# Linear attention's gate pair moved behind the other input pairs, and the output projection's Strassen gemms rearranged

## The chip, the cores and the metric

The kernel runs on one core of one Trainium2 chip. The metric is device time of one execution in microseconds; the kernel before took 1664.3 us (median of three runs, 1661.51 to 1664.69). The engines are PE (TensorE: matmuls and transposes), DVE (VectorE), ACT (ScalarE), POOL (GpSimd, which here mostly issues DMAs) and SP (SyncE, which only issues DMAs). Each engine works through its own list of instructions in order.

## What is computed

Two layers over 512 tokens of width 2048, float32. Each layer normalises its rows, multiplies by one wide input matrix, splits the columns between a linear-attention group (GLA, 4 heads) and a chunked-attention group (8 heads), gates each group, multiplies by one output matrix, normalises again and adds to the residual:

```python
def hybrid_layer(x, w_in, w_out, g_pre, g_post, w_alpha, b_alpha, g_gla, g_att, rel_bias):
    h = rmsnorm(x, g_pre)
    z = h @ w_in
    gq, gk, gv, gg, ga, aq, ak, av, ag = split_columns(z)
    log_a = jax.nn.log_sigmoid((ga @ w_alpha + b_alpha).astype(jnp.float32)) / GLA_TAU
    o_gla = gla_chunk_causal(gq.reshape(...), gk.reshape(...), gv.reshape(...), log_a.reshape(...))
    o_gla = rmsnorm(o_gla, g_gla.reshape(GLA_HEADS, GLA_DV)).reshape(B, S, D_GLA)
    o_gla = o_gla * jax.nn.silu(gg)
    o_att = chunk_band_attention(aq.reshape(...), ak.reshape(...), av.reshape(...), rel_bias)
    o_att = rmsnorm(o_att, g_att.reshape(ATT_HEADS, ATT_HD)).reshape(B, S, D_ATT)
    o_att = o_att * jax.nn.silu(ag)
    y = jnp.concatenate([o_gla, o_att], axis=-1) @ w_out
    return x + rmsnorm(y, g_post)
```

## The kernel before

*Matmuls.* Both projections are cut into blocks of 512 columns and run with operands split in a high and a low part (`split`, L105), three matmuls per product of tiles. A block over all four groups of 128 tokens takes 192 matmuls of 128x512 in the plain form (`std_gemm`). `fast_gemm` (L311) computes a pair of blocks by a Strassen-like scheme with 7 products of half size, 28 jobs of 12 matmuls, 336 in place of 384. `PROD` and `PROD_END` are the order of the jobs; "51" means product P5, chunk c=1 of the inner dimension. The products read tokens' half matrices or sums of them (S1 to S4); the sums are formed once, written to DRAM and read back into the ring `sa` when a job wants them.

*Jobs.* Every job has a weight tile, either one block's (512 KB, `raw` or `H`) or a sum of two formed on DVE (L180, L182). ACT casts it into `wh` (four buffers), DVE forms the rest `wl` (three buffers, L194). `ahead` prepares loads 5 jobs, casts 4 jobs and splits 3 jobs in advance of the matmuls.

*Side work.* Everything between the gemms (token sums, attention heads, GLA heads, output sums, finishing of rows) is written as generators in the list `tasks`; each gemm calls `pump` a given number of times per job (`rate`), and `until` pumps until a condition holds. These generators only set the order in which instructions are handed over; a scheduler of the framework then fixes the order on each engine. Side work on PE writes to the four PSUM banks of `ps_ax`; the gemms accumulate in the four of `ps_mm`. Small tiles come from `t2`, eight buffers.

*A layer.* Input blocks in this order: the attention gates AG0 and AG1 in plain form, then six Strassen pairs (`PAIRS`, L126): GG (the GLA gate), AV, two QK pairs, KQ of the GLA group, GV. The gates are passed through SiLU and stored to DRAM (`gate`, L710). The GLA heads (`Unit`) run after GV; each loads its gate tile (in `states`), multiplies while it evicts (L1121), is transposed on PE (L1131), scaled on ACT (L1142), stored (L1146) and split into an output operand. `output_sums` (L545) reads these halves back (L549, L553) and forms S1 to S4 for each chunk of the output's inner dimension (L527 to L536, `put` with the store at L518).

*The output.* Blocks 0 and 1 in plain form, blocks 2 and 3 (`W23`) as a Strassen pair with `end=True`, in which P2 has an accumulator of its own in two `ps_ax` banks. In layer 0 block 1 is cut: tokens 0 to 255 before the pair and 256 to 511 after it, so that the rows of the first half are finished under the last gemm. `finish` normalises and adds the residual rows; in layer 0 it also prepares the next layer's operands.

Of the kernel before, what the change touches and what calls it, by code (L numbers as in the profile page):

```python
# [15 lines left out]
P = 128  # L16
L = 2
# [16 lines left out]
def hybrid_trunk(  # L34
# [59 lines left out]
    sg_d = [[dram([S, 1024], f"sg{l}{h}") for h in range(2)] for l in range(L)]  # L94
# [31 lines left out]
    PAIRS = ((GG0, GG1), (AV0, AV1), (QK01, QK23), (QK45, QK67), (GK, GQ), (GV0, GV1))  # L126
    W23 = (NB_IN + 2, NB_IN + 3)
# [8 lines left out]
    class Job:  # L136
# [14 lines left out]
        def load(self):  # L151
            k, c, p, b0, b1 = self.kind, self.c, self.pair, self.b0, self.b1
            end = b0 == W23[0]
            top, bottom = (c + 4, c) if end else (c, c + 4)
            if k == "std":
                self.raw = self.fetch(rtile("raw"), b0, c)
            elif k == "P1":
                p["H", c] = self.fetch(rtile("H"), b0, top)
            elif k == "P5":
                p["r", c] = self.fetch(rtile("raw"), b1, top)  # L160
            elif k == "P6":
                p["r", c] = self.fetch(rtile("raw"), b1, bottom)
            elif k == "P7":
                p["r", c] = self.fetch(rtile("raw"), b0, top)
            elif k == "P2" or (k == "P4" and end):
                p["r", c] = self.fetch(rtile("raw"), b0, bottom)
            src = (so_d if end else sa_d)[self.l].get((LEFT.get(k), c))
            if src is not None and not (k == "P5" and b0 == GG0):
# [3 lines left out]
        def high(self):  # L172
# [3 lines left out]
            else:  # L176
                h, r = p["H", c], p.get(("r", c))
                src = h if k in ("P1", "P5", "P6", "P4") else r
                if k in ("P5", "P6") or (k == "P4" and self.b0 == W23[0]):
# [11 lines left out]
        def low(self):  # L191
# [5 lines left out]
            if self.kind == "P2" and self.b0 != W23[0]:  # L197
# [4 lines left out]
    for l in range(L):  # L202
# [39 lines left out]
    delayed = []  # L242

# [67 lines left out]
    def fast_gemm(l, pair, consume, rate=0.0, skip=0, feature_major=False, after=None, end=False, lag=0):  # L311
# [38 lines left out]
        def matmuls(job, k, c, ts):  # L350
            a = job.a
            if a is None:
                a = A[{"P1": (0, 0, c), "P2": (1, 0, c), "P4": (1, 1, c), "P5": ("S1", c)}[k]]
            out_ps = acc[target[k]]
            fresh = k in starts and c == 0
            for kk in range(2):
                if feature_major:
                    for ft in range(4):
# [3 lines left out]
                        ops = ((job.wh, 0), (job.wh, 1), (job.wl, 0))  # L362
                        for m, (lhs, part) in enumerate(ops):
# [5 lines left out]
                else:  # L369
                    for t in ts:  # L370
                        tok = slice(kk * 256 + t * P, kk * 256 + (t + 1) * P)
                        ops = ((0, job.wh), (0, job.wl), (1, job.wh))
                        for m, (part, rhs) in enumerate(ops):
# [60 lines left out]
    STAGE = ("g16", "g17", "g4", "g5", "g10")  # L434
    HOME = {("S1", c): tag for c, tag in enumerate(("g9", "g14", "g15", "g2"))}
    XS0 = (("g6", "g7"), ("g12", "g13"))
# [25 lines left out]
    def prep_half(l, half, xs):  # L462
# [10 lines left out]
        h_end = next((i for i, z in enumerate(stream) if z.l == l - 1 and z.b0 == W23[0] and z.kind == "P4"), 0) + 1  # L473
# [32 lines left out]
    def make_sums(dst, tags, parts, home={}, chunks=range(4)):  # L506
        stage = [0]

        def put(name, c, src):
# [8 lines left out]
            nc.gpsimd.dma_start(dst[name, c], flat(op))  # L518

# [162 lines left out]
    def load_forget_gate(l):  # L682
        wga = [slot(tag, [n, 96], F32R) for tag, n in (("g6", 10), ("g7", 6))]
# [24 lines left out]
    def layer(l):  # L708
        last = l == L - 1
        def gate(half, q, t, src, scale=1.0):  # L710
            dst = t2()
            nc.scalar.activation(dst, src, AF.Silu, scale=scale)
            nc.gpsimd.dma_start(sg_d[l][half][t * P : (t + 1) * P, q * W : (q + 1) * W], dst)

        def gate_evac(half, q):
            def f(o, ps):
                gate(half, q, o, ps)
            return f

        def gate_consume(j, h, t, src, comb):  # L720
            gate(0, j, 2 * h + t, settled(src, comb))
# [94 lines left out]
        def raw_evac(o, ps):  # L816
            gate(1, 0, o, ps, r0[:, o : o + 1])

        if l:
            std_gemm(l, AG0, (0, 1), CO, operand_in, gate_evac(1, 0), rate=1.2)  # L820
            tasks.append(token_sums(l))
            tasks.append(forget_gate())
            std_gemm(l, AG0, (2, 3), CO, operand_in, gate_evac(1, 0), rate=0.8)
            std_gemm(l, AG1, range(NT), CO, operand_in, gate_evac(1, 1), rate=1.3, lag=2)
# [550 lines left out]
```

## Time and profile before

| | us |
|---|---|
| median of three runs | 1664.3 |
| lowest and highest of them | 1661.51 and 1664.69 |
| span of the profiled execution, first to last instruction | 1661.4 |
| layer 0, gate pair (102.71 to 178.87) | 76.16 |
| layer 0, output block 0 (631.29 to 700.86) | 69.57 |
| layer 0, first half of block 1 | 21.76 |
| layer 0, pair of blocks 2 and 3 | 79.79 |
| layer 0, second half of block 1 (802.41 to 827.76) | 25.35 |
| layer 1, output blocks 0 and 1 (1462.01 to 1568.92) | 62.71 and 44.20 |
| layer 1, pair of blocks 2 and 3, to its last matmul (1649.23) | 80.31 |
| from there to the end | 12.21 |

The profiler gives no other time of the profiled execution than its span. Stages are cut at the first matmul of each gemm. In a row of windows the columns are the stretch, its length, then for each engine the time it was busy and the number of instructions, the granted TensorE clock, the share of the 16 DMA engines that was busy and the rate. In a row of groups the numbers are: count, total busy time, mean duration in ns, and the engine's idle time just before, with what ended it. In a timeline row they are start, length, engine, line, operation, output and inputs, with the idle time before in brackets. In a row of DMA issues the last number is the median time to landing.

### The profile page before, as it was taken

What the parts mean: (1) busy time and instruction counts of PE and PEld (TensorE: products, weight loads), DVE (VectorE), ACT (ScalarE), POOL (GpSimd) and SP (SyncE); (2) the same over time, 40 slices, a digit from 0 to 9 for tenths busy, and PEclk for the clock granted to TensorE, in tenths of its full rate; (3) what the DMA queues carried; (4) which work ended last, traced back from release to release, by engine and by line L of the source; (5) the groups of instructions that cost most, each with busy time, mean ns of one, the idle gap of its engine ahead of it and who ended that gap; (6) DMA issues with size and microseconds to landing.
All of it is one profiled execution on the core that took longest, in us unless ns stands there. A gap on an engine that the chain in (4) does not pass through costs nothing.

```text
span 1661.4 us, 24811 instructions
## 1 busy us (share of the span) xinstructions
PE 1631.3 (98%) x9034; PEld 1393.9 (84%) x9034; DVE 1223.0 (74%) x1603; ACT 873.0 (53%) x1441; POOL 166.5 (10%) x252
## 2 busy tenths in 40 slices
PE   9999999999999999899999999999999999999996
PEld 7888889999988877688788888799999888777884
DVE  5977777787767876678886577667878678754778
ACT  7544544465665544454874445344656655343552
POOL 0110000000101101310122000000001011012103
PEclk9999999999999999999999999999999999999999
DMA  8898785858758777898789487868587687865975
GB/s 341 275 344 309 276 328 207 313 173 308 253 207 297 260 297 253 319 340 304 266 289 390 165 323 267 322 203 300 178 307 253 208 289 265 325 211 197 360 281 207
DMA packets 143722, 457.39 MB, mean 275 GB/s; under 512 B 15524, under 2 KB 32292, under 8 KB 143600
## 3 DMA queue, kind: packets, MB, share of 16 engines
q1 hardware_dynamic: 120848, 376.32, 63.9%
q0 software_dynamic: 22176, 78.41, 12.2%
q8 instruction: 71, 1.16, 0.3%
q10 hardware_dynamic: 576, 1.08, 0.2%
q14 instruction: 51, 0.42, 0.1%
HBM read 383.64 MB, written 72.11 MB: 274 GB/s over the span
## 4 chain that ended last, share of the span: by engine, by line
PE 85%; issue 6%; DMA 4%; DVE 3%; ACT 1%; POOL 1%; SPq 0%; DVEq 0%; POOLq 0%; ACTq 0%
PE mm L374 37%; PE mm L297 19%; PE mm L364 18%; PE ax L915 2%; DMA raw<-in_w_dram 2%; DVE wl L194 1%; PE ax L1069 1%; PE ax L898 1%; PE ax L1103 1%; PE ax L734 1%; DMA sa<-S 1%; PE ax L374 1%; DMA oS<-g 1%; PE ax L879 1%; PE ax L878 1%
## 5 line engine op out<-in xcount | busy, mean ns | idle before, releaser
L374 PE MATMUL mm<-wh,sa 128*128 128x512 f32 x1472 | 471.0, 392 | 3.2 <-DMA sa<-S 3.2
L186 ACT CAST wh<-raw 128x1024 fp32r<-128x1024 f32 (+1 forms) x249 | 260.8, 1051 | 273.0 <-PE mm L374 67.7
L194 DVE TENSOR_TENSOR wl<-raw,wh 128x1024 fp32r<-128x1024 f32 (+1 forms) x249 | 302.3, 1218 | 96.3 <-PE mm L374 37.1
L186 ACT CAST wh<-H 128x1024 fp32r<-128x1024 f32 x224 | 234.8, 1051 | 217.8 <-PE mm L374 98.7
L194 DVE TENSOR_TENSOR wl<-H,wh 128x1024 fp32r<-128x1024 f32 x224 | 273.3, 1222 | 86.8 <-PE mm L374 30.9
L374 PEld LDWEIGHTS mm<-wh,sa 128*128 128x128 f32 x1472 | 276.3, 188 | 62.7 <-DMA sa<-S 2.5
L374 PE MATMUL mm<-wl,sa 128*128 128x512 f32 x736 | 287.9, 391 | 0.0
L364 PE MATMUL mm<-sa,wh 128*128 128x256 f32 x1280 | 236.6, 285 | 0.0
L364 PEld LDWEIGHTS mm<-sa,wh 128*128 128x128 f32 x1280 | 199.5, 191 | 0.2
L374 PE MATMUL mm<-wh,a 128*128 128x512 f32 x576 | 189.7, 393 | 0.0
L364 PE MATMUL mm<-sa,wl 128*128 128x256 f32 x640 | 181.6, 284 | 0.6 <-DVE wl L194 0.6
L374 PEld LDWEIGHTS mm<-wl,sa 128*128 128x128 f32 x736 | 138.3, 188 | 28.5 <-issue 0.8
L180 DVE TENSOR_TENSOR H<-H,raw 128x1024 f32<-128x1024 f32 x120 | 145.7, 1221 | 9.3 <-DMA raw<-in_w_dram 8.2
L297 PE MATMUL mm<-wh,a 128*128 128x512 f32 x448 | 148.2, 395 | 3.1 <-ACT a L106 2.2
L416 POOL TENSOR_TENSOR sm<-sm,mhalf 128x2 f32<-128x2 f32 (+2 forms) x42 | 58.8, 1402 | 676.9 <-DVE sm L925 458.2
L374 PEld LDWEIGHTS mm<-wh,a 128*128 128x128 f32 x576 | 107.5, 188 | 21.8
L364 PEld LDWEIGHTS mm<-sa,wl 128*128 128x128 f32 x640 | 122.5, 191 | 1.2 <-DVE wl L194 1.0
L182 DVE TENSOR_TENSOR raw<-H,raw 128x1024 f32<-128x1024 f32 x56 | 68.6, 1225 | 73.1 <-DMA raw<-in_w_dram 72.8
L374 PE MATMUL mm<-wl,a 128*128 128x512 f32 x288 | 113.6, 394 | 0.0
L297 PEld LDWEIGHTS mm<-wh,a 128*128 128x128 f32 x448 | 83.8, 188 | 23.3 <-ACT a L106 2.6
L297 PE MATMUL mm<-wh,g 128*128 128x512 f32 x272 | 95.0, 398 | 2.2 <-ACT g L106 2.2
L297 PE MATMUL mm<-wh,sa 128*128 128x512 f32 x288 | 96.1, 396 | 1.0 <-ACT wh L186 0.6
(219 smaller groups left out, 2421.4 us busy)
## 6 DMA issues: line engine op xcount, KB each, us to landing
raw<-in_w_dram SPq DMA_DIRECT2D x311, 512.0 KB, 5.3
sa<-S SPq DMA_DIRECT2D x184, 512.0 KB, 4.4
H<-in_w_dram SPq DMA_DIRECT2D x56, 512.0 KB, 5.3
sa<-A SPq DMA_DIRECT2D x48, 512.0 KB, 5.9
S<-g POOLq DMA_DIRECT2D x32, 512.0 KB, 9.6
sa<-oS SPq DMA_DIRECT2D x32, 512.0 KB, 5.0
oS<-g POOLq DMA_DIRECT2D x24, 512.0 KB, 7.5
sg<-t POOLq DMA_DIRECT2D x32, 256.0 KB, 6.3
```

The costliest lines, as they stand in the source:

```text
L180: nc.vector.tensor_tensor(out=h, in0=h, in1=r, op=ALU.add)
L182: nc.vector.tensor_tensor(out=r, in0=h, in1=r, op=ALU.subtract)
L186: last_cast[0] = nc.scalar.copy(self.wh[:, z, :], src[:, z, :]).ins
L194: nc.vector.tensor_tensor(out=self.wl[:, z, :], in0=self.src[:, z, :], in1=self.wh[:, z, :].bitcast(F32), op=ALU.subtract)
L297: nc.tensor.matmul(pss[o], a(part, kk, o) if callable(a) else a[:, part, t], rhs[:, kk, :], start=(i == 0 and kk == 0 and m == 0), stop=(i ...
L364: nc.tensor.matmul(dst, lhs[:, kk, f], a[:, part, tok], start=(fresh and kk == 0 and m == 0 and ft % 2 == 0), stop=(c == 3 and kk == 1 and ...
L374: nc.tensor.matmul(out_ps[t], a[:, part, tok], rhs[:, kk, :], start=(fresh and kk == 0 and m == 0), stop=(c == 3 and kk == 1 and m == 2), ...
L416: nc.gpsimd.tensor_tensor(out=out_r, in0=v, in1=mhalf[:, : v.shape[-1]], op=ALU.pow)
L734: nc.tensor.matmul(ps[0:96, half * 256 : (half + 1) * 256], wga[kt // 10][:, kt % 10, :], op[:, i, (kt % 2) * 256 : (kt % 2 + 1) * 256], s ...
L878: nc.tensor.matmul(ps[:, :n], self.qh[:, t], self.kl[:, :n], start=False, stop=False)
L879: nc.tensor.matmul(ps[:, :n], self.ql[:, t], self.kh[:, :n], start=False, stop=True)
L915: nc.tensor.matmul(o, self.pt[i][:, j * P : (j + 1) * P], av[hd // 4, j // 2][:, j % 2, (hd % 4) * P : (hd % 4 + 1) * P], start=(j == 0), ...
```

## The change

1. The order of the input pairs: GG, which was the first Strassen pair, becomes the last, after GV. `W01` (blocks 0 and 1 of the output) becomes a Strassen pair with `end=True`.
2. The GLA heads no longer load a gate tile. `evict` (on ACT) writes the normalised head into `normed`; when the gate pair's product arrives, `gg_consume` applies SiLU and multiplies `normed` in place on DVE, and `turn_gla` transposes, stores and splits as `turn` did, two or three pumps later. Heads 2 and 3 take part with j=1 (products P3 and P7), heads 0 and 1 with j=0 (P2 and P4). The gate no longer goes through DRAM.
3. The output runs `W01` by Strassen in both layers. In layer 1 `W23` follows by Strassen as well; in layer 0 blocks 2 and 3 run in plain form, each half of the tokens on its own (four gemms of 96 matmuls).
4. Output chunks are taken in the order `OC` = (2, 3, 0, 1). `output_sums` is handed over ahead of the gate pair for all four chunks and waits for the heads; a job's load of a sum first waits until that sum has been issued. The sum tiles are g0 to g3, one buffer each, in both layers.
5. The residual rows are loaded by a task of their own. Several tiles have other slots.

```diff
-    PAIRS = ((GG0, GG1), (AV0, AV1), (QK01, QK23), (QK45, QK67), (GK, GQ), (GV0, GV1))
-    W23 = (NB_IN + 2, NB_IN + 3)
+    PAIRS = ((AV0, AV1), (QK01, QK23), (QK45, QK67), (GK, GQ), (GV0, GV1), (GG0, GG1))
+    W01, W23 = (NB_IN, NB_IN + 1), (NB_IN + 2, NB_IN + 3)
+    OC = (2, 3, 0, 1)
...
+                until(lambda: k == "P4" or (id(sums), LEFT[k], c) in written)
                 self.a = rtile("sa", (2, 512), F32R)
                 nc.sync.dma_start(flat(self.a), src)
...
-        for b in (NB_IN, NB_IN + 1):
-            stream += [Job(l, "std", c, b) for c in OO]
-        pr = {}
-        stream += [Job(l, k, c, *W23, pr) for k, c in PROD_END]
+        for b0, b1 in (W01, W23) if l == L - 1 else (W01,):
+            pr = {}
+            stream += [Job(l, k, c, b0, b1, pr) for k, c in PROD_END]
         if l < L - 1:
-            stream += [Job(l, "std", c, NB_IN + 1) for c in OL]
+            stream += [Job(l, "std", c, b) for half in range(2) for b in W23 for c in OL]
...
-            def gate(self):
+            def evict(self):
+                h, p = self.h, self.p
+                if h >= 2:
+                    if (2, p) not in normed:
+                        z = slot(f"g{16 + p}", [2, 2, 256])
+                        normed[2, p], normed[3, p] = z[:, :, 0, :], z[:, :, 1, :]
+                else:
+                    tag = ("bias", "sg")[h]
+                    normed[h, p] = tmp.tile([P, 2, 256], F32, tag=tag, name=nm(tag), bufs=2)
                 for tt in range(2):
-                    nc.vector.scalar_tensor_tensor(
-                        out=self.sg[:, tt, :], in0=self.ps_o[:, tt * 256 : (tt + 1) * 256],
-                        scalar=self.r[:, tt : tt + 1], in1=self.sg[:, tt, :], op0=ALU.mult, op1=ALU.mult,
+                    nc.scalar.activation(
+                        normed[h, p][:, tt, :], self.ps_o[:, tt * 256 : (tt + 1) * 256], AF.Copy,
+                        scale=self.r[:, tt : tt + 1],
                     )
...
+        fast_gemm(l, PAIRS[4], gv_consume, rate=2)
+        act_table("silu_and_others")
+
+        def gg_consume(j, h, t, src, comb):
+            until(lambda: len(gla_done) == 4)
+            sg = t2()
+            nc.scalar.activation(sg, settled(src, comb), AF.Silu)
+            for i in range(2):
+                dst = normed[2 * j + i, h][:, t, :]
+                nc.vector.tensor_tensor(out=dst, in0=dst, in1=sg[:, i * 256 : (i + 1) * 256], op=ALU.mult)
+                if t:
+                    delayed.append([2 + i, lambda hd=2 * j + i: turn_gla(hd, h)])
+
+        tasks.append(output_sums(l, OC, output_ready, ("g0", "g1", "g2", "g3")))
+        fast_gemm(l, PAIRS[5], gg_consume, rate=3, after=fetch_operands)
...
+        fast_gemm(l, W01, out_consume(0), rate=3, end=True, ops=O)
+        drain()
         if last:
-            std_gemm(l, NB_IN + 1, range(NT), OO, operand_out, out_evac(1), rate=0.8, lag=2)
+            fast_gemm(l, W23, out_consume(2), rate=3, end=True, lag=3, ops=O)
         else:
...
+            for half in range(2):
+                for b in W23:
+                    std_gemm(l, b, (2 * half, 2 * half + 1), OL, operand_out, out_evac(b - NB_IN), rate=3, lag=2)
```

The scheduler's order on VectorE in layer 0, from the split of W01's third job in its list (P1 c=1, `wl_1273`) to the gate product of the last heads, in the built program (line, operation, output and inputs with buffer numbers and shape):

```
L199 TensorTensor wl_1273_6691<-H_1261_6625,wh_1271_6675 128x1024
L107 TensorTensor g5_1230_6462<-t2_1231_6463,g5_1230_6462 128x512
L185 TensorTensor H_1255_6589<-H_1255_6589,raw_1323_6873 128x1024
L199 TensorTensor wl_1295_6762<-raw_1272_6677,wh_1274_6693 128x1024
L535 TensorTensor t2_1228_6452<-t2_1227_6451,t2_1228_6452 128x512
L199 TensorTensor wl_1303_6797<-H_1275_6695,wh_1296_6764 128x1024
...
L199 TensorTensor wl_1312_6833<-raw_1297_6766,wh_1304_6799 128x1024
...
L1221 TensorTensor bias_1166_6180<-bias_1166_6180,t2_1276_6697 128x256
L1221 TensorTensor sg_1199_6316<-sg_1199_6316,t2_1276_6697 128x256
```

Further down the same list, around the first sum of chunk 0 (`g0_1288`; `wl_1365` is the split for P5 c=3, `sa_1342` the ring tile that P5 c=2 reads):

```
L199 TensorTensor wl_1365_7047<-H_1305_6801,wh_1362_7029 128x1024
L107 TensorTensor g7_1286_6730<-t2_1287_6731,g7_1286_6730 128x512
L535 TensorTensor t2_1284_6720<-t2_1283_6719,t2_1284_6720 128x512
L185 TensorTensor H_1305_6801<-H_1305_6801,raw_1367_7052 128x1024
L538 TensorTensor t2_1283_6719<-t2_1281_6717,t2_1283_6719 128x512
L107 TensorTensor g0_1288_6738<-t2_1284_6720,g0_1288_6738 128x512
```

More of the change, by code (lines that the diff above doesn't have):

```diff
@@ L242, in hybrid_trunk @@
     delayed = []
+    written = set()
     def pump(n):
@@ L472, in prep_half @@
         base = l * 2 * KT
-        h_end = next((i for i, z in enumerate(stream) if z.l == l - 1 and z.b0 == W23[0] and z.kind == "P4"), 0) + 1
+        h_end = next((i for i, z in enumerate(stream) if z.l == l - 1 and z.b0 == W01[0] and z.kind == "P4"), 0) + 1
         for ch in CO:
@@ L1313, in layer @@
-        for c in range(4):
-            del A[1, 1, c]
-        drain()
-        if not last:
-            tasks.append(finish(1, xs1))
+            for half in range(2):
+                for b in W23:
+                    std_gemm(l, b, (2 * half, 2 * half + 1), OL, operand_out, out_evac(b - NB_IN), rate=3, lag=2)
+                    if half == 0 and b == W23[0]:
+                        for i in range(4):
+                            op_att[1, i] = rtile("sa", (2, 512), F32R)
+                            nc.sync.dma_start(flat(op_att[1, i]), oa_d[l][1, i])
+                if half == 1:
+                    drain()
+                tasks.append(finish(half, xs[half]))
```

192 lines of the change are left out of this document (86 added, 106 removed).

## The prediction

> **What bounds the kernel now.** I read the page first, then the busy time of each engine in windows cut at the first matmul of each gemm, then single shapes, DMA landings and a timeline of the stretch the change rebuilds.
>
> ```profile
> span 1661.4 us, 24811 instructions
> PE 1631.3 (98%) x9034; PEld 1393.9 (84%) x9034; DVE 1223.0 (74%) x1603; ACT 873.0 (53%) x1441; POOL 166.5 (10%) x252
> PE 85%; issue 6%; DMA 4%; DVE 3%; ACT 1%; POOL 1%; SPq 0%; DVEq 0%; POOLq 0%; ACTq 0%
> ```
>
> TensorE (PE) is busy 98% of the span and carries 85% of the chain that ended last, so time follows its matmuls unless something makes it wait. The three runs lie at 1661.51 to 1664.69 us; the profiled execution's span, 1661.4 us, is 2.9 us under their median. I sum changes against the span and add 2.9.
>
> ```profile
> core 0: us, PE busy (x) PEld busy (x) DVE busy (x) ACT busy (x) POOL busy (x), PEclk, DMA share, GB/s
> 102.71:178.87 76.16, 76.16 (x337) 63.06 (x336) 56.55 (x51) 36.91 (x42) 4.87 (x9) 1.00 0.85 322
> 631.29:700.86 69.57, 65.17 (x332) 47.89 (x330) 42.06 (x77) 31.12 (x75) 19.78 (x32) 0.98 0.84 299
> 700.86:722.62 21.76, 21.76 (x98) 18.02 (x96) 14.80 (x18) 11.95 (x15) 2.14 (x4) 1.00 0.87 287
> 722.62:802.41 79.79, 77.18 (x337) 62.79 (x336) 69.37 (x74) 44.11 (x61) 10.67 (x15) 1.00 0.89 338
> 1462.01:1524.72 62.71, 61.80 (x332) 45.41 (x330) 33.42 (x61) 26.31 (x65) 15.79 (x24) 1.00 0.60 202
> 1524.72:1568.92 44.20, 43.83 (x193) 35.96 (x192) 27.21 (x36) 17.79 (x30) 5.88 (x11) 1.00 0.84 307
> ```
>
> Rows in order: layer 0's gate pair; its output block 0; half of block 1; the Strassen pair of blocks 2 and 3; layer 1's blocks 0 and 1. The gate pair has 336 matmuls, no side work and no idle: 76.16/336 = 0.227 us a matmul, 2.72 us a Strassen job of 12. (A duration of 390 ns overlaps its neighbours; the pace is what counts.) Blocks 0 and 1 are the only stretches where VectorE (DVE) is near half empty (42 of 70, 33 of 63, 27 of 44 us). There the kernel hides the last heads, the transposes and the output sums.
>
> **The change: what it saves.** Layer 0 keeps its matmul count: 192+192+336 = 720 before, 336+4x96 = 720 after. Layer 1 goes from 720 to 672: 48 x 0.227 = **-10.9 us**. Layer 0's block 0 lost 69.57-65.17 = 4.4 us waiting for late head operands plus some 1.4 at a lower clock (rows below); this gemm is gone, **-5.8**. Layer 1's blocks lost 0.91+0.37: **-1.3**. A Strassen output pair takes 79.79 against 76.16 because DVE is late at its end; layer 0 has one such pair before and after, layer 1 gets a second, without the finishing of rows in it: **+3**.
>
> **What it adds beside other work.** Twenty more weight jobs (8 in layer 0, 12 in layer 1), each a cast and a split:
>
> ```profile
> L194 DVE TENSOR_TENSOR wl<-raw,wh 128x1024 fp32r<-128x1024 f32 x247 | 300.9, 1223 | 96.1 <-PE mm L374 37.1 <-PE mm L297 23.1 <-PE mm L364 19.0
> L107 DVE TENSOR_TENSOR g<-t,g 128x512 fp32r<-128x512 f32 x36 | 24.4, 689 | 5.5 <-ACT g L106 5.4
> L1121 DVE SCALAR_TENSOR_TENSOR bias<-ax,sm,bias 128x256 f32<-128x256 f32 x16 | 7.0, 481 | 2.3 <-POOL sm L416 2.3
> 709.20 0.69 DVE L527 TENSOR_TENSOR t<-t,t 128x512 f32<-128x512 f32 x1 [2.83 <-DMA t<-fg]
> 709.80 1.22 DVE L194 TENSOR_TENSOR wl<-raw,wh 128x1024 fp32r<-128x1024 f32 x1
> 710.94 0.69 DVE L530 TENSOR_TENSOR t<-t,t 128x512 f32<-128x512 f32 x1
> ```
>
> The last three rows give the start-to-start cost, a little under the duration: 0.60 us for 512 columns, 1.14 for 1024; 256 columns I take at 0.40 (the pair at 689.71 in the next fence takes 0.87 us with 0.48 each). A job is 2.72 us of PE, so in the late standard blocks of layer 0 these 1.14 us hide completely. The gate's stores and reloads through DRAM (16 transfers of 256 KB a layer) go, hidden before: 0. The gate products move to TENSOR_TENSORs, the evictions to ACT (53% busy, and one more table load): under other work, 0. The head's work on PE is the same and only moves under the gate pair: 0. Side work that loses its cover is the next part.
>
> **What loses its cover.** Before, from the last head's gate to the Strassen pair's first use of its sum there lay a whole block and more. I followed that chain in layer 0 (DVE gate; ACT copies of the transposes; POOL store; SP reload; DVE sum and split; POOL store; SP load into `sa`):
>
> ```profile
> 689.71 0.87 DVE L1121 SCALAR_TENSOR_TENSOR sg<-ax,sm,sg 128x256 f32<-128x256 f32 x2
> 693.17 1.56 ACT L1142 ACTIVATE t<-ax,gcol 128x256 f32<-128x256 f32 x4
> 694.69 1.08 POOL L1146 DMA_DIRECT2D fg<-t  x2 [0.23 <-issue]
> 700.40 0.53 SPq L549 DMA_DIRECT2D t<-fa  x1
> 712.52 0.54 POOL L518 DMA_DIRECT2D oS<-g  x1 [16.76 <-DVE g L107]
> 716.75 0.92 SPq L170 DMA_DIRECT2D sa<-oS  x1
> oS<-g POOLq DMA_DIRECT2D x24, 512.0 KB, 7.5
> sa<-oS SPq DMA_DIRECT2D x32, 512.0 KB, 5.0
> DMA to landing us min/median/max: 3.1/6.0/13.9
> ```
>
> From 689.71 to 716.75, plus 5.0 for the last load, is 32 us. (The landing row is that of all `oS` transfers.) After the change the same chain starts at the end of the gate pair (call that T0, the first matmul of W01), because heads 0 and 1 are gated only by its last product. In W01 the first sum of these chunks is wanted by the twelfth job, P5 with c=2, at T0+11x2.72 = T0+30, or T0+32 with the 16 transposes that stand in between (about 0.11 us each, by the two rows of four in the last fence). So even if the gate came at T0+3 and nothing was in the way, PE would wait about 3 us there. But much is in the way, as the order in which the built program puts instructions on the engines shows (its VectorE part stands with the change, above).
>
> *First wait, at W01's start.* All four banks for side work are taken by the four transposes of the last heads, so P2, which wants two of them for its accumulator, cannot start before these are read. PE's order therefore is P1 c=0, 1, 2, a bit of c=3, six transposes (one each of the second half's), then P2. These transposes wait for the gate products, and those wait for `t2` buffers (eight, all held by the sums of chunks 2 and 3). On DVE there stand from T0 (the split of the third job needs a buffer that the gate pair's last job frees) to the product wanted: 7 operations of 1024 columns, 13 of 512, 6 of 256: 8.0+7.8+2.4 = 18.2 us. PE has work for 9.3 (three jobs, two matmuls, six transposes). Lower bound 8.9; with the waits for freed `wl` buffers and for stores of the single-buffered sum tiles I take **11**, upper bound 15.
>
> *Second wait, P5 c=2.* DVE's order puts the sum for it behind the split of the job two further on, whose buffer (three in all) is freed when PE finishes the job just before P5 c=2. So PE runs out first, and only then come split, turn, sum, add, sum, split: 2x1.14+4x0.60+0.1 = 4.8 us, POOL's issue 0.6, the store 7.5 and the load 5.0: **17.9**, by the rows' medians. Both transfers at 3.1 give 11.6; the store at 13.9 gives 24.3. While PE waits no weights are loaded, so I take 17. *Third wait, P5 c=3*: its sum is written to the same tile as the one before, after that one's store landed, and its own store runs while PE has two jobs: 7.5-5.4 and a split more, **3** (0 to 8). SP holds everything behind these loads; the weights for the jobs to P6 c=3 stand ahead of them, so no more is added.
>
> Sum of a layer: 11+17+3 = 31; two layers **+62** (bounds 2 x (8.9+11.6) = 41 and 2 x (15+24+8) = 94). In layer 1 W23's first accumulator is the one W01 used last, **+1**.
>
> *After a wait PE is slow:*
>
> ```profile
> 687.63 0.80 PE L297 MATMUL mm<-wh,g 128*128 128x512 f32 x1 [2.16 <-ACT g L106]
> 688.22 0.63 PE L297 MATMUL mm<-wl,g 128*128 128x512 f32 x1
> 690.78 0.93 PE L297 MATMUL mm<-wh,g 128*128 128x512 f32 x3
> 691.55 0.40 PE L297 MATMUL mm<-wl,g 128*128 128x512 f32 x1
> 691.79 0.39 PE L297 MATMUL mm<-wh,g 128*128 128x512 f32 x1
> 692.02 0.60 PE L1131 MATMUL ax<-cst,bias 128*128 128x128 f32 x4
> 692.45 0.60 PE L1131 MATMUL ax<-cst,sg 128*128 128x128 f32 x4
> 695.29 0.50 PE L297 MATMUL mm<-wh,a 128*128 128x512 f32 x1 [2.23 <-ACT a L106]
> ```
>
> After 2.16 us idle the next seven went at 0.43 us (688.22 to 690.78 is six steps), 7x0.2 = 1.4 us; after the 2.23 us at 695.29 none did. Two long waits a layer: 4x1.4 = **+5.6**, bounds 0 and 10. The Trainium skill speaks against the change here: its page "TensorE: Matmul & The Clock Gate", section "What's actually happening", says that an idle window of about 3.4 us halves the array's clock until it has been busy for as long. The rows agree on the halved pace, though not on how long it takes to lose it. By that page, an estimate, each long wait costs 1.7 us and the term would be 6.8.
>
> Sum: -10.9-5.8-1.3+3+62+1+5.6 = +53.6; 1661.4+53.6+2.9 = 1717.9, forecast **1718 us**.
>
> **Rivals.**
> 1. *All stays covered* (faster). The sums of chunks 2 and 3 are ready early, P1 and P2 need none, and before PE never waited for `oS`. If the 30 us suffice, what is left is -10.9-5.8-1.3+3 = -15: **1649**. It decides if the chain from the last gate takes under 30 us; the rows give 32 at best, with none of the queueing. Against it.
> 2. *The waits come at their lower bounds*: transfers land in 3.1 us since PE's idling empties the queues, DVE never waits, no slow clock: 41-15+1: **1691**. For it: landings of 3.1 in the row. Against: four stores of the sums leave together, and residual rows share POOL's queue.
> 3. *Transfers saturate*: the sums' 12.6 MB (16 stores of 512 KB, 16 loads of 256 KB) fall on gemms that already move 322 to 338 GB/s at shares of 0.85 to 0.89 (first and fourth window row); waits at their upper bounds, 94+10-15+1 = +90: **1754**. Against it: residual rows are issued early, and the waits themselves relieve the queues.
> 4. *Nothing to be seen*: savings and waits cancel, waits of 7 us a layer, -15+14+1 = 0: **1664**; needs the waits at a quarter of their size.
>
> **How the numbers follow.** Forecast (waits of 25 to 40 us a layer) 0.62; rival 1 0.11; rival 2 0.13; rival 3 0.10; rival 4 0.04. About 0.2% (3.3 us) is what can be told from no change. Faster 0.11, same 0.04, slower 0.85. The range goes down to 1682, between rivals 2 and 4, and up to 1745, short of rival 3's bound; below lie rivals 1 and 4 (0.15), above some 0.05.
>
> **What would show it.** In the profile after, PE's idle time should sit in the first third of W01 in both layers: one wait of about 11 us before transposes, released by DVE or ACT, and one of about 17 us before the matmul that reads `sa`, released by the load of `sa<-oS`, then a short one on the same. DVE's share there should be high before the first wait, low in the second. The other gemms should keep 0.227 us a matmul, and layer 0's four standard halves should show no idle. It is wrong if W01 runs near 78 us, if PE waits on weights (`raw`, `wl`) rather than on the sums, or if the gate pair itself stretches.

## The result, and the profile after

| | us |
|---|---|
| before, median of 4 runs | 1662.9 (1658.97 to 1664.69) |
| after, median of 4 runs | 1701.0 (1699.57 to 1704.44) |
| ratio after to before | 1.0231, 95% interval 1.0213 to 1.025 |
| span of the profiled execution, before and after | 1661.4 and 1698.4 |

The change makes the kernel 38.1 us slower by the medians, 37.0 us by the spans of the two profiled executions. 1718 us was predicted, with a range of 1682 to 1745.

The head of the page of after, with the shares of the chain of work that ended last:

```profile
span 1698.4 us, 24821 instructions
PE 1628.3 (96%) x8986; PEld 1389.0 (82%) x8986; DVE 1267.1 (75%) x1647; ACT 912.5 (54%) x1502; POOL 156.4 (9%) x236
PE 85%; DMA 6%; issue 5%; DVE 2%; POOL 1%; ACT 0%; SPq 0%; DVEq 0%; POOLq 0%; ACTq 0%
```

PE has 48 instructions fewer, as the diff says, and is busy 3 us less, in a span 37 us longer. Windows of after, cut at the first matmul of each gemm (columns as before). Rows in order: layer 0's gate pair, its W01, its first standard half; layer 1's gate pair, its W01, its W23 to the end. The last fence has the W23 of layer 1 before.

```profile
core 0: us, PE busy (x) PEld busy (x) DVE busy (x) ACT busy (x) POOL busy (x), PEclk, DMA share, GB/s
555.80:648.45 92.65, 92.65 (x461) 70.65 (x460) 68.34 (x88) 50.15 (x89) 12.82 (x17) 1.00 0.80 279
648.45:759.44 110.99, 84.69 (x354) 67.76 (x352) 85.26 (x102) 54.87 (x81) 12.96 (x25) 0.89 0.90 327
759.44:781.20 21.76, 21.76 (x98) 18.03 (x96) 12.60 (x13) 10.01 (x14) 0.00 (x0) 1.00 0.65 206
1401.74:1495.31 93.57, 92.87 (x461) 70.66 (x460) 68.53 (x88) 50.05 (x89) 11.93 (x17) 1.00 0.80 276
1495.31:1605.57 110.26, 84.42 (x353) 67.85 (x352) 85.41 (x102) 55.12 (x81) 12.96 (x25) 0.88 0.93 340
1605.57:1698.40 92.83, 77.58 (x337) 62.60 (x335) 71.70 (x75) 38.05 (x54) 11.04 (x9) 0.95 0.61 213
```

```profile
1568.92:1661.40 92.48, 77.25 (x337) 62.64 (x335) 75.88 (x82) 39.76 (x57) 15.42 (x14) 0.96 0.69 256
```

All of the loss lies in W01. At full pace its 336 matmuls and 16 transposes take 336x0.227 + 16x0.113 = 78.1 us; it took 111.0 and 110.3, an excess of 32.9 and 32.2. PE is idle 26.3 and 25.8 us of that. The rest is mostly slow matmuls: the granted clock is 0.89 and 0.88 there, 1.00 in the gate pairs and the standard half. The gate pairs hide the head's work as they should. One sum the prediction did not make is in these rows: VectorE (DVE) is busy 85 us in W01, longer than PE's 78.1 at full pace.

Where PE stood still in layer 0's W01, from PE's timeline (start, length, engine, line, operation, tiles, and in brackets the idle time before with what ended it; L381 is the Strassen matmul, L1139 a transpose of a gated head, L1221 the gate product):

```profile
656.16 0.50 PE L381 MATMUL mm<-wl,a 128*128 128x512 f32 x1 [1.66 <-DVE wl L199]
659.92 0.73 PE L381 MATMUL mm<-wh,a 128*128 128x512 f32 x2 [1.18 <-ACT wh L191]
663.08 0.45 PE L1139 MATMUL ax<-cst,bias 128*128 128x128 f32 x1 [2.42 <-DVE bias L1221]
667.96 0.45 PE L1139 MATMUL ax<-cst,bias 128*128 128x128 f32 x1 [2.76 <-DVE bias L1221]
669.01 0.63 PE L381 MATMUL ax<-wl,g 128*128 128x512 f32 x1
669.44 1.06 PE L381 MATMUL ax<-wh,g 128*128 128x512 f32 x2
688.82 0.47 PE L381 MATMUL mm<-wh,sa 128*128 128x512 f32 x1 [1.78 <-DMA sa<-oS]
694.14 0.39 PE L381 MATMUL mm<-wh,sa 128*128 128x512 f32 x1
709.36 0.77 PE L381 MATMUL mm<-wh,sa 128*128 128x512 f32 x1 [14.84 <-ACT g L106]
709.93 0.63 PE L381 MATMUL mm<-wl,sa 128*128 128x512 f32 x1
710.36 1.05 PE L381 MATMUL mm<-wh,sa 128*128 128x512 f32 x2
712.91 0.77 PE L381 MATMUL mm<-wh,sa 128*128 128x512 f32 x2
718.54 0.47 PE L381 MATMUL mm<-wh,sa 128*128 128x512 f32 x1 [1.66 <-DMA sa<-oS]
```

The three predicted waits are there, and a short one that was not predicted: 1.78 us at 688.82, before the matmul of P5 c=1 that reads its loaded sum. The first came in four pieces, 8.0 us, the last two released by gate products on DVE; the second is 14.84 us before the matmul that reads `sa` (its releaser is named as ACT, a cast of another sum that this matmul does not read; the load below explains it, and the same wait in layer 1, 15.58 us, is put down to the load); the third is 1.66. What happened in the second wait stands in the timelines of DVE (first fence), POOL (second) and SP (third):

```profile
694.41 1.23 DVE L199 TENSOR_TENSOR wl<-H,wh 128x1024 fp32r<-128x1024 f32 x1 [1.50 <-ACT g L106]
695.55 0.69 DVE L107 TENSOR_TENSOR g<-t,g 128x512 fp32r<-128x512 f32 x1
696.15 0.69 DVE L535 TENSOR_TENSOR t<-t,t 128x512 f32<-128x512 f32 x1
696.75 1.22 DVE L185 TENSOR_TENSOR H<-H,raw 128x1024 f32<-128x1024 f32 x1
697.89 0.69 DVE L538 TENSOR_TENSOR t<-t,t 128x512 f32<-128x512 f32 x1
698.49 0.69 DVE L107 TENSOR_TENSOR g<-t,g 128x512 fp32r<-128x512 f32 x1
```

```profile
699.49 0.55 POOL L525 DMA_DIRECT2D oS<-g  x1 [4.70 <-DVE g L107]
```

```profile
702.79 1.31 SPq L175 DMA_DIRECT2D sa<-oS  x2
```

PE starts its last matmul at 694.14. DVE then does split, turn, sum, add, sum, split, the order that the prediction lists; POOL stores the sum at 699.49, SP loads it at 702.79, and PE goes on at 709.36. Further up this chain, POOL issued the store of the turned head that chunk 0's sum reads at 678.15, and SP its reload only at 687.28, when the store had landed.

### The profile page after: what moved, and what is told of

It is laid out like the page before. It is cut to its first block, busy times and chain, and to the rows that moved or that the text cites. A ratio compares the mean times of both kernels' runs of the same rounds, so it can differ in the third digit from the quotient of the medians.

```text
span 1698.4 us, 24821 instructions
## 1 busy us (share of the span) xinstructions
PE 1628.3 (96%) x8986; PEld 1389.0 (82%) x8986; DVE 1267.1 (75%) x1647; ACT 912.5 (54%) x1502; POOL 156.4 (9%) x236
## 4 chain that ended last, share of the span: by engine, by line
PE 85%; DMA 6%; issue 5%; DVE 2%; POOL 1%; ACT 0%; SPq 0%; DVEq 0%; POOLq 0%; ACTq 0%
PE mm L381 42%; PE mm L371 18%; PE mm L302 15%; PE ax L919 2%; DMA oS<-g 1%; DMA sa<-oS 1%; DMA raw<-in_w_dram 1%; PE ax L1101 1%; PE ax L902 1%; PE ax L739 1%; PE ax L1073 1%; DVE wl L199 1%; DMA t<-fg 1%; PE ax L381 1%; DMA bias<-in_rel_dram 1%
## 5 line engine op out<-in xcount | busy, mean ns | idle before, releaser
L381 PE MATMUL mm<-wh,sa 128*128 128x512 f32 x1600 | 521.9, 397 | 35.9 <-DMA sa<-oS 21.0
L381 PEld LDWEIGHTS mm<-wh,sa 128*128 128x128 f32 x1600 | 302.2, 189 | 110.3 <-ACT g L106 31.2
L191 ACT CAST wh<-H 128x1024 fp32r<-128x1024 f32 x240 | 251.6, 1051 | 224.3 <-PE mm L381 111.5
L199 DVE TENSOR_TENSOR wl<-H,wh 128x1024 fp32r<-128x1024 f32 x240 | 292.9, 1222 | 100.7 <-PE mm L381 44.4
L381 PE MATMUL mm<-wl,sa 128*128 128x512 f32 x800 | 314.9, 394 | 0.0
L381 PE MATMUL mm<-wh,a 128*128 128x512 f32 x608 | 200.9, 395 | 3.1 <-ACT wh L191 2.4
L381 PEld LDWEIGHTS mm<-wl,sa 128*128 128x128 f32 x800 | 151.4, 189 | 29.4
L185 DVE TENSOR_TENSOR H<-H,raw 128x1024 f32<-128x1024 f32 x132 | 160.6, 1220 | 11.1 <-DMA raw<-in_w_dram 9.8
L381 PEld LDWEIGHTS mm<-wh,a 128*128 128x128 f32 x608 | 113.2, 188 | 27.4 <-ACT wh L191 4.3
L381 PE MATMUL mm<-wl,a 128*128 128x512 f32 x304 | 119.9, 394 | 3.2 <-DVE wl L199 3.2
L371 PE MATMUL mm<-a,wh 128*128 128x256 f32 x512 | 95.1, 286 | 0.0
L302 PE MATMUL mm<-wh,a 128*128 128x512 f32 x288 | 91.8, 390 | 0.0
L333 ACT COPY ev<-mm 128x512 f32<-128x512 f32 x96 | 55.9, 583 | 58.0 <-PE mm L381 41.2
```

The source lines that it names most:

```text
L185: nc.vector.tensor_tensor(out=h, in0=h, in1=r, op=ALU.add)
L191: last_cast[0] = nc.scalar.copy(self.wh[:, z, :], src[:, z, :]).ins
L199: nc.vector.tensor_tensor(out=self.wl[:, z, :], in0=self.src[:, z, :], in1=self.wh[:, z, :].bitcast(F32), op=ALU.subtract)
L302: nc.tensor.matmul(pss[o], a(part, kk, o) if callable(a) else a[:, part, t], rhs[:, kk, :], start=(i == 0 and kk == 0 and m == 0), stop=(i ...
L333: nc.scalar.copy(e, src[t])
L371: nc.tensor.matmul(dst, lhs[:, kk, f], a[:, part, tok], start=(fresh and kk == 0 and m == 0 and ft % 2 == 0), stop=(c == 3 and kk == 1 and ...
```

## The experiments

Three accounts were set against each other. A is the prediction's: three waits, each with its own cause, that add up. B: one chain from the last gate to the loaded sum. C: W01's transfers, 36 MB a layer, fill its time. Times without an interval are of one run; W01's lengths are from that run's profile, cut at its first matmul. The edits are shown in their main lines. All runs but the one with the residual rows, the one with cover and the first of the versions at the end also have the later transposes of the first edit.

**Transposes later.** The turning of heads 0 and 1 is asked for fourteen steps later, behind P2's first jobs:

```
-   delayed.append([2 + i, lambda hd=2 * j + i: turn_gla(hd, h)])
+   delayed.append([2 + i + (0 if j else 14), lambda hd=2 * j + i: turn_gla(hd, h)])
```

> The transposes of heads 0 and 1 are asked for fourteen steps later, so that P2 gets its two banks before them; no work is left out. Theory A (the prediction: three separate waits, the long one because the sum of chunk 0 stands on VectorE behind a split that PE itself frees): the first wait (8.9 us) and its slow matmuls (1.7) go, the long wait at P5 c=2 keeps its 15 us, W01 falls from 111 to about 100 us in both layers, total about 1680 us. Rival B (one chain from the last gate decides when the sum of chunk 0 is in, and the waits before it only share that time out): the idle time moves to P5 c=2, which waits 22 to 24 us, W01 stays at 108 to 111 us, total 1696 to 1701. Rival C (W01's transfers, 36 MB, fill the time): W01 110 us, total 1700.

1700.5 us; W01 111.3 and 111.5. From PE's timeline of this run:

```profile
686.17 0.80 PE L381 MATMUL mm<-wh,sa 128*128 128x512 f32 x1 [5.64 <-DMA sa<-oS]
```

```profile
711.60 0.76 PE L381 MATMUL mm<-wh,sa 128*128 128x512 f32 x1 [16.94 <-DMA sa<-oS]
```

The first wait shrinks to about half (2.1, 2.0 and 0.8 us from matmul to matmul are left), and the time comes back before the loads of sums. The two waits are 22.6 us together, in the 22 to 24 that B asked for at one place. So the waits do not add: A falls. What PE reaches sooner it waits for longer. The edit did not delay the chain itself: the head's store went out 29.4 us after W01's start (29.7 without the edit), and its reload 38.8 us after it (38.8).

**Sums from heads that are ready early.** The sums of chunks 0 and 1 read the stored rows of heads 2 and 3, which leaves out their dependence on heads 0 and 1:

```
-   nc.sync.dma_start(tiles[2 * half + 1], of_gla[l][half, c])
+   nc.sync.dma_start(tiles[2 * half + 1], of_gla[l][half, c % 2 + 2])
```

> As the run before, and the sums of chunks 0 and 1 read the stored rows of heads 2 and 3 in place of heads 0 and 1 (wrong operands, the same number of loads, sums, stores and bytes), so no sum depends on the last gate. Theory A and rival B: no long wait is left, PE idles under 6 us a layer in W01, W01 at 78 to 86 us, total 1640 to 1655. Rival C: the 36 MB still have to pass at some 330 GB/s, W01 stays above 100 us, total above 1680.

1694.2 us; W01 103.9 and 107.3. The experiment had a flaw of its own: with all sums ready, they were put on DVE ahead of the gate products, and PE waited some 19 us before a transpose, released by a gate product. It was repeated with those sums behind the gate products:

```
-   return 2 * c in heads_done and (0, c % 2 + 2) in og and (1, c % 2 + 2) in og
+   return 2 * c in heads_done and (c > 1 or len(gated) == 8) and (0, c % 2 + 2) in og and (1, c % 2 + 2) in og
```

> The early-heads experiment again, with its flaw mended: the sums of chunks 0 and 1 again read the stored rows of heads 2 and 3 (wrong operands, same work and bytes), but are asked for only after the last gate products, so these aren't held up on VectorE; transposes late as in the first run. Rival B: no chain is left, PE idles under 8 us a layer, W01 at 80 to 90 us, total 1645 to 1665. Rival C: 36 MB at 340 to 400 GB/s, W01 at 92 to 105 us, the idle time spread over several loads, total 1670 to 1690.

1693.6 us; W01 106.6 and 106.0. Its window and PE's longest wait:

```profile
649.79:756.37 106.58, 86.70 (x354) 69.23 (x353) 83.74 (x102) 53.99 (x81) 12.99 (x25) 0.87 0.94 338
```

```profile
687.04 0.76 PE L381 MATMUL mm<-wh,sa 128*128 128x512 f32 x1 [10.66 <-DMA sa<-oS]
```

With no sum reading the last heads, W01 is only about 5 us shorter than with the later transposes alone (4 to 7 in the run before). The longest wait now stands before P5 c=1, a sum of chunk 3, whose heads were gated early: its load was issued at 678.89 and let PE go on at 687.04, in a stretch where the DMA share is 1.04. So the sums of chunks 2 and 3 come late as well. Two limits remain: here the sums of chunks 0 and 1 were still asked for behind the last gate products, and in the run before the gate products were late, so no run has both early. And C, which asked for more than 100 us in the first of these runs and 92 to 105 in the second, comes nearer to both than A or B, which asked for at most 90.

**Shorter way for the sums of chunks 0 and 1.** The turned head stays in SBUF for the sum, and S1 stays there for P5:

```
-   full_o = t2()
+   full_o = full_gla[p, h]        # for h < 2, a slot of its own
...
-   tiles[2 * half + 1] = t2(), loaded from of_gla
+   tiles[2 * half + 1] = full_gla[half, c]
...
+   OHOME = {("S1", 0): "a122", ("S1", 1): "a123"}
```

> As the first run, and for chunks 0 and 1 the sums read the turned head from SBUF (no store and reload of it) and S1 stays in SBUF for W01's P5 (no load; its store stays). Theories A and B: the three transfers of the chain are gone, S1 of chunk 0 is ready at about T0+36, just when PE wants it; waits of 0 to 6 us a layer, W01 at 78 to 86 us, total 1640 to 1655. Rival C: W01 moves about 4 MB less and takes about 98 us, total about 1675.

1681.5 us, W01 103.0 and 98.5: 8 and 13 us gained on the later transposes alone, where A and B asked for 25 to 33. What is left in layer 0 are four waits, 15.1 us in all, each ended by a load of a sum.

**Loads that wait for no sum.** W01 loads the sums of the input gemms instead, stored long before; in the second run layer 0 also leaves out the stores:

```
+   if src is not None and b0 == W01[0]:
+       src = sa_d[self.l][LEFT[k], c]
...
+   if dst is not so_d[0]:
        nc.gpsimd.dma_start(dst[name, c], flat(op))
```

> W01's loads into `sa` (P5, P6, P3, P7) read the sums that the input gemms stored long before (wrong operands, the same 16 loads of 512 KB); the output sums are still made and stored, so the bytes are the same, but no load and no matmul of W01 waits for them. Transposes late as in the first run, so what is left of the chain is the gate products for P2 and P4. Rival B (the way from gate to loaded sum is what PE waits for): PE idles under 6 us a layer in W01, W01 79 to 86 us, total 1640 to 1652. Rival C (the bytes that W01 moves fill its time): W01 90 to 104 us, idle time before loads of `sa` or weights, total 1665 to 1690.

> As the run before, and in layer 0 alone the 16 stores of the output sums (8.4 MB) are left out; layer 1 keeps them. Rival B: layer 0's W01 as in the run before, within 2 us. Rival C: 36 MB become 28, layer 0's W01 is 10 to 20 us shorter than in the run before and near 80 us, layer 1's W01 stays.

1675.4 and 1668.6 us. Windows of W01 in both layers, first of the run with the stores, then of the run without them in layer 0:

```profile
649.63:743.15 93.52, 83.96 (x354) 66.58 (x352) 81.82 (x100) 52.29 (x81) 13.47 (x25) 0.96 0.98 379
1482.91:1577.34 94.43, 83.18 (x353) 64.86 (x351) 83.60 (x104) 54.02 (x86) 13.47 (x25) 0.98 1.01 390
```

```profile
650.22:742.03 91.81, 82.74 (x353) 63.85 (x352) 83.20 (x102) 54.50 (x83) 4.90 (x9) 1.00 0.83 298
1478.70:1574.09 95.39, 83.81 (x353) 65.24 (x352) 83.25 (x101) 54.38 (x83) 13.47 (x25) 0.96 1.00 386
```

Waiting for sums is worth 17 to 18 us of W01 (111.3 to 93.5, 111.5 to 94.4); B asked for 25 to 32. The W01 that remains fits C's span of times, but not its cause: 8 MB fewer shorten layer 0's W01 by only 1.7 us, though the DMA share falls from 0.98 to 0.83 (layer 1's W01, the same in both runs, differs by 1.0). What full queues add to the waits themselves this pair can't say, as no load waits for a sum in either. What is left, 91.8 against 78.1, goes in part with DVE, busy 83.2 of 91.8 us. Of PE's 9.1 us of idle there, these waits are released by DVE (us in total, times, longest; L201 is the split, L1224 the gate product):

```profile
PE mm L383 <- DVE wl L201: 4.7, 6, 1.6
PE ax L1142 <- DVE bias L1224: 1.4, 2, 0.8
```

The other 3.0 us of idle are three waits on ACT and one on a load, and the rest of the 13.7 is slow matmuls. No run took DVE's work on sums away by itself.

**Residual rows later.** Their loading was moved behind W01 in the program:

```
-   tasks.append(residual_rows())
    fast_gemm(l, W01, out_consume(0), rate=3, end=True, ops=O)
+   tasks.append(residual_rows())
```

> The residual rows (4.2 MB a layer, read from DRAM beside W01, wanted only when rows are finished) are loaded behind W01 in place of beside it; nothing else changes. Rival B (the chain from the last gate through transposes, store, reload, sum, store and load sets the end of the wait): these rows are not on the chain, W01 stays at 106 to 110 us, total 1692 to 1701. Rival C (W01's transfers fill its time): 4.2 of 36 MB fewer at some 340 GB/s are 12 us a layer, W01 at 97 to 100 us, total 1677 to 1682.

1704.5 us, W01 111.9. This run tells nothing: the rows depend on nothing, the scheduler issued them where they had been, and W01 moved 36.3 MB as before. Only 1 of the 4.2 MB had lain in W01 at all.

**Cover in front of W01.** In layer 0 the two standard halves of tokens 0 to 255 run ahead of W01:

```
+   if not last:
+       for b in W23:
+           std_gemm(l, b, (0, 1), OO, operand_out, out_evac(b - NB_IN), rate=3, lag=2)
    fast_gemm(l, W01, out_consume(0), rate=3, end=True, ops=O)
```

> In layer 0 the two standard halves for tokens 0 to 255 of blocks 2 and 3 (43.5 us of PE, attention chunks first) run ahead of W01 in place of behind it; layer 1 is untouched. Theories A and B: the chain is covered in layer 0, its W01 takes 78 to 80 us, layer 0 loses 31 to 33 us, total 1668 to 1672 us; layer 1's W01 keeps 110 us. Rival C: W01 in layer 0 has fewer stores beside it but stays above 90 us, total above 1680.

1680.9 us, 1.011 of before (1.0078 to 1.0143). Windows of the first half, the second, W01, and the unchanged W01 of layer 1:

```profile
650.49:678.03 27.54, 25.66 (x113) 20.74 (x112) 23.75 (x35) 19.17 (x30) 6.63 (x14) 0.94 1.00 360
678.03:699.80 21.77, 21.77 (x98) 18.02 (x96) 12.21 (x12) 10.09 (x12) 2.07 (x4) 1.00 1.03 409
699.80:779.92 80.12, 77.25 (x338) 62.76 (x336) 73.93 (x81) 43.55 (x63) 9.55 (x18) 1.00 0.94 348
1472.81:1583.56 110.75, 85.65 (x354) 68.68 (x352) 84.95 (x102) 54.81 (x81) 12.96 (x25) 0.88 0.93 332
```

W01 falls to 80.1 us in layer 0 and stays at 110.8 in layer 1, as expected; the expected total of 1668 to 1672 was missed. Much of the sums' work on DVE (W01 keeps DVE busy 74 us now, not 85) and of their transfers lies under the two halves, which run at DMA shares of 1.00 and 1.03; the first of them pays 5.8 us for it, 1.8 of these for the 16 transposes that moved to it (so W01 at full pace would be 76.3 here, not 78.1). Some 4 us more are spread over other gemms of that execution. So the total fell by 20 and not by 31.

**Versions meant to beat both.** The first has the last layer's blocks 0 and 1 plain again (with layer 0 as in the last run); the second has the last layer all by Strassen with the direct sums, the later transposes and the later rows. The edit of the first; that of the second is the edits above together, the direct sums in the last layer alone:

```
+   if last:
+       for b in W01:
+           std_gemm(l, b, range(NT), OO, operand_out, out_evac(b - NB_IN), rate=3, lag=2)
+   else:
        fast_gemm(l, W01, out_consume(0), rate=3, end=True, ops=O)
```

> Layer 0 as in the run with the standard halves first; in the last layer blocks 0 and 1 are plain again and W23 alone goes by Strassen, with the gate pair still last of the inputs. 48 matmuls come back (10.9 us), the waits of W01 (25 us idle and some 7 us of slow matmuls) go: two plain blocks of 43.6 us each in place of 110.8. Total 1655 to 1662, that is 0.1 to 0.5% under the kernel before. If the chain or the transfers only move into W23, its 92 to 94 us grow by 10 or more and the total stays above 1668.

> Layer 0 with the standard halves first; last layer all by Strassen with what helped before: transposes later, sums of chunks 0 and 1 straight from SBUF with S1 kept there, residual rows behind W01. Rival B: W01 of the last layer as in the direct run, 96 to 100 us, total 1664 to 1670. Rival C: its 34.4 MB fall to some 30, W01 at 85 to 90 us, total 1654 to 1660.

1671.4 us, 1.0053 of before (1.0037 to 1.007), and 1673.9 us, 1.0063 (1.0044 to 1.0081). In the first the last layer's two plain blocks take 57.8 and 43.5 us, with 8.0 us of idle, 6.0 of it before transposes; in the second its W01 still takes 104.2, though the same edit gave 98.5 there in the direct run: single profiles of W01 can differ by that much. Both missed their forecasts (1655 to 1662, and 1654 to 1670). The plain version was carried on, first with later transposes (the edit of the first experiment), then with the output sums asked for only behind the gate pair:

```
-   tasks.append(output_sums(l, OC, output_ready, ("g0", "g1", "g2", "g3")))
    fast_gemm(l, PAIRS[5], gg_consume, rate=3, after=fetch_operands)
    A.clear()
+   tasks.append(output_sums(l, OC, output_ready, ("g0", "g1", "g2", "g3")))
```

> The version with the standard halves first in layer 0 and plain blocks 0 and 1 in the last layer, with the transposes of heads 0 and 1 asked for fourteen steps later, so that they stand behind the six chunks whose operands are ready (16 us of PE). Its 8.0 us of idle before transposes in the last layer's block 0 and 1.9 us in layer 0's first half should go, with some 3 us of slow matmuls: total 1657 to 1662, against 1671 without; 0.0 to 0.4% under the kernel before. If the gate products are not ready after 16 us either, the wait stays at 3 to 6 us and the total at 1664 to 1668.

> As the run before with plain blocks in the last layer and later transposes, and the output sums are asked for only after the gate pair, so that no sum of chunks 2 and 3 stands ahead of the gate products on VectorE or holds their buffers. If these sums are what keeps the gate products (and with them the transposes) late, as the prediction's first wait has it: the 6.7 us wait in the last layer's block 0 goes, with its slow matmuls, the block falls from 54.6 to 45.5 to 48 us, layer 0's first half from 25.3 to 23.6, total 1656 to 1660, 0.2 to 0.4% under the kernel before. If the products are late for another reason, the wait stays and the total at 1664 to 1667; if the later sums are missed instead, W01 of layer 0 or W23 grow by as much.

1666.5 us, 1.0025 of before (1.0014 to 1.0036), and 1665.5 us, 1.002 (1.0005 to 1.0035). PE's wait in the last layer's block 0, from the timelines of these two runs:

```profile
1486.89 0.45 PE L1143 MATMUL ax<-cst,bias 128*128 128x128 f32 x1 [6.26 <-DVE bias L1229]
```

```profile
1526.28 0.79 PE L306 MATMUL mm<-wh,a 128*128 128x512 f32 x1 [5.31 <-DVE a L1264]
```

Later transposes did not end the wait for the gate products; asking for the sums behind them, which takes the sums off DVE and out of the shared buffers ahead of them, did. So the sums were what held the gate products back, as the prediction's first wait has it; which of the two, DVE's time or the buffers, stays open. But the sums then stand ahead of the block's evictions (`a`, L1264), and the next block's first matmul waits 5.3 us for these instead; layer 0's two standard halves grow from 47.0 to 50.8 us as well. The first came out at the time forecast for a wait that stays, the second missed the 1656 to 1660 forecast for one that goes. None of the versions is faster than the kernel before.

## Why the prediction was right, and where its steps were not

*Direction and place: right.* The loss is in W01 of both layers, the other gemms keep their pace (layer 0's value pair takes 76.16 us before and after, and layer 0's standard halves show no idle), and the rivals without a loss (1 and 4) fell. By the number alone rival 2, 1691, lies nearer to 1701 than the forecast does, but not for its reasons: the waits came to 54.4 us, not 41, and the slow matmuls, which it left out, cost 10.6. Credits 14 us larger than either sum has bring the total down (below).

*What W01 costs: right as a total, 67.6 us predicted, 32.9 + 32.2 = 65.1 measured, and partly by luck: the waits came 7.6 us lower than forecast, the slow matmuls 5.0 higher.* Its terms, per layer:

| term | predicted | after, layer 0 and layer 1 |
|---|---|---|
| first wait | 11 | 8.8 and 9.3 |
| second wait | 17 | 16.9 and 15.7 |
| third wait | 3 | 1.8 and 1.9 |
| slow matmuls | 2.8 | 5.4 and 5.2 |

(From matmul to matmul, less the normal step; the second wait of layer 0 with the 1.9 us at 688.82. The rows add up to 32.9 and 32.1; the slow matmuls are what is left of the total.) The first lies at its lower bound. Of the second, the store took 3.3 us (699.49 to 702.79), not 7.5, and load and start 6.6 (702.79 to 709.36), not 5.0; DVE's part is 699.18 less 694.41, 4.8 as predicted.

*The mechanism: right in what ended each wait, wrong in what the waits mean.* The step "11+17+3" treats them as separate; the first experiment took half of the first away and W01 stayed as long. The step that names heads 0 and 1, gated by the last product, as the origin holds only in part: without the sums' dependence on these heads W01 is about 5 us shorter, where the second and third wait, 17 and 3, were put down to it. The prediction's cover argument sees one chain of 32 us. What the runs showed in its place is a whole stage without cover: all sixteen sums, with a store and a load each, are made and fetched within the gemm that reads them. For layer 0's W01, run by run:

| W01 of layer 0 | us |
|---|---|
| as changed; with later transposes | 111.0; 111.3 |
| sums depend on early heads only | 106.6 |
| loads wait for no sum | 93.5 |
| and no sum is stored | 91.8 |
| sums made beforehand, under other matmuls | 80.1 |
| matmuls alone, at full pace | 78.1 |

About 5 us go with the way from the last heads to their sums, 13 with the rest of the wait for sums, 2 with the bytes of the stores. Between 91.8 and 80.1 lie 12: 1.8 are the transposes, which moved out with the sums, and the other 10 are put down here to DVE's work on sums beside its splits and gate products, which is argued from its busy time and not tested alone. (The rows are not strictly nested; each is one profile.) The prediction's "these 1.14 us hide completely" holds for each job, not for the stage: with the sums in it W01 gives DVE 85 us of work, and its 78 us of PE can't cover that.

*Slow matmuls: undersized.* The seven slow steps that were predicted after a long wait came: from 709.93 to 712.91 are seven of 0.43 us. What was left out is the first step after each wait (0.57 us at 709.36, not 0.23) and the transposes behind the first wait, which ran at half pace too, 1.1 us in each layer. The Trainium skill's "TensorE: Matmul & The Clock Gate", section "What's actually happening", has the clock halved by an idle window of some 3.4 us until PE has been busy for as long. The 3.6 us from 709.36 to 712.91 agree with it, and so do the waits of 1.78 and 1.66 us at 688.82 and 718.54, behind which the steps are 0.31 and then 0.24 us. The first wait does not agree: after pauses of 1.66, 1.18 and 2.42 us, none of them 3.4, the transposes from 663.08 already run at half pace (0.33 and 0.24 us a step, not 0.11).

*What was to show it.* Idle time before transposes and before loads of `sa`: there. "In the first third": the long wait lies at 41 to 55% of W01. DVE's share "low in the second": wrong, as the windows of 10 us in the first and in the second wait show:

```profile
659.00:669.00 10.00, 3.89 (x13) 2.64 (x14) 10.00 (x19) 7.74 (x15) 4.82 (x9) 0.65 0.99 326
699.00:709.00 10.00, 0.00 (x0) 0.00 (x0) 7.47 (x13) 3.81 (x9) 2.15 (x4) 0.53 0.85 297
```

DVE is full in the first and still at 0.75 in the second, with the sums. The first row also has the transfers at 0.99: rival 3's saturation is there for a while; single transfers took longer there (last section), but the waits stayed far below its upper bounds, 54.4 us in all against 94.

*The credit side: this is what put 1718 above 1701.* Predicted -10.9-5.8-1.3+3+1 = -14.0, measured 37.0 - 65.1 = -28.1.
- Layer 1's gate pair and two blocks: 76.45 + 62.70 + 44.20 = 183.4 before, 93.57 + 78.1 = 171.7 after without W01's excess: -11.7, predicted -10.9-1.3 = -12.2. Right.
- "Layer 0 has one such pair before and after": wrong. The pair's 3.6 us of lateness at its end (79.79 against 76.16) does not appear in W01, which has no wait after 718.54; no finishing of rows lies in it, which may be why. With that and 1.5 us more, which is what remains and may be fewer and faster side matmuls, layer 0 gained 10.9 where 5.8 was predicted.
- "Layer 1 gets a second", +3, and +1 for the accumulator: did not come; W23 takes 92.83 against 92.48.
- Some 6 us are small stalls of layer 1's input gemms in the profile of before that the one of after lacks. One of them, the value pair, took 78.26 us before; it took 76.4 here, 76.3 and 78.6 in two of the experiments. So this one comes and goes between executions; for the others that is not shown.

## What to carry to other kernels

Moving a stage to the end takes away the cover of all that hangs on it: count not only the latest chain but all work of each engine (sums, splits, products, stores, loads) against the PE time of the gemm that must hide it. Waits that follow each other need not be a sum: take one away and see whether the next grows before crediting it. Putting matmuls that need nothing new in front (43.5 us of standard halves here) made W01 31 us shorter where it was done and cost 6 of them in the halves; shortening the path itself brought 8 to 13, and 6 in the version that had it in one layer.

## What the runs showed of the hardware

With sums, weights and reloads together the 16 DMA engines ran for a whole half block (21.8 us) at a share of 1.03 and 409 GB/s, above the 322 to 338 GB/s of the gemms quoted before. How long one transfer takes beside the others shows in after, in two stretches of W01 (DMA issues: count, KB, median us to landing), first 655 to 690 us, with a DMA share of 0.98, then 690 to 712, most of it the second wait, with 0.70:

```profile
oS<-g POOLq DMA_DIRECT2D x8, 512.0 KB, 7.4
sa<-oS SPq DMA_DIRECT2D x3, 512.0 KB, 10.9
```

```profile
oS<-g POOLq DMA_DIRECT2D x6, 512.0 KB, 4.5
sa<-oS SPq DMA_DIRECT2D x2, 512.0 KB, 7.5
```

The counts are small. The same load took a median of 5.0 us over the whole of the kernel before. A median over a span is a poor price for a transfer in its fullest stretch.
